# First layer of a two-layer backbone: ten more first-product blocks made in the gate stage (80 spilled in place of 70), the loop projects that many fewer

## The chip, the cores and the metric

The kernel runs on one core of one Trainium2 chip. Its time is the device time of one execution in microseconds (us), given as the median of several runs. Engines are named as the profile names them: PE is TensorE, DVE is VectorE, ACT is ScalarE, POOL is GpSimd and SP is SyncE, which here only issues transfers.

## The reference, cut to what matters

Two layers act on 512 latent tokens and 256 context tokens of width 1024. Each layer has a token mixer (convolution, gating and attention heads, one output projection) and then a channel mixer that looks up experts; the change lies in the channel mixer of the first layer. There every token picks 16 of 16,384 experts for each of 8 heads, and

```
a   = gelu(einsum('tkd,td->tk', u_tab[ec], xc))    # first product: picked rows of u times the token
out = einsum('tk,tkd->td', a * gc, v_tab[ec])      # second product: gated sum of the picked rows of v
```

where `ec` holds the 128 picked experts of a token and `gc` their softmax gates.

## The kernel before, in words

For the 512 latent tokens of the first layer the kernel computes both products for all experts and not for the picked ones: the 16,384 experts are 128 blocks of 128, and a dense matrix of gates, zero where an expert was not picked, takes the place of the lookup. The 256 context tokens are done by lookup. For each of 512 jobs one indirect transfer on POOL (line 842) gathers 128 rows of 4 KB, and DVE multiplies or accumulates them (lines 847 and 858).

A **first product** (`u_phase`, line 828) is one block of 128 experts times all 512 tokens. SP loads 512 KB of `u`, ACT splits off the high part (line 163, tile `whi`), DVE makes the low part (line 164, `wlo`), PE runs 24 matmuls (lines 315 to 317), and ACT applies the gelu (line 831, tile `a`). For a block that is to be spilled ACT's queue then sends `a`, 256 KB, to the DRAM tensor `ad`.

The channel mixer of the layer has three stretches. In the **lead-in** the tail of the expert choice (many small DVE instructions) runs beside first products. In the **gate stage** 32 steps build the dense gates: in each, DVE makes two one-hot tiles (lines 989 and 990, `oj` and `oi`) and two weighted ones (line 994, `wo`), PE runs 32 short matmuls (line 1002), ACT evicts them twice (line 1004), and 1 MB goes to the DRAM tensor `gd`. First products run between the steps. In the **loop**, 16 groups of 8 expert blocks pass. For each block `prep` (line 1042) needs `a`: a spilled one is read back from `ad`, one of the three carried ones (`CARRY`) is still on the chip, any other is a first product made now. DVE multiplies it with the gates (line 1056), ACT and DVE split it (lines 1061 and 1062), and PE runs 8 second products of 24 matmuls for the group (lines 1098 to 1100), after each of which DVE adds into the stream (line 1101, `x_l`). The gates of the next group, 2 MB, are read from `gd` once in a group.

Which blocks are spilled is worked out from `AHEAD`: as many of the 128 as it says, evenly spread. Spilled and carried blocks are made in this order by `upto` (line 898), which is called in the expert choice (20 blocks, `AHP`) and after every gate step, up to `AHP` and then a share of `AHT` that grows with the step to the power 1.3 (line 1010). The same call hands out the gather jobs, 112 before the loop. The 400 that are left are handed out in the loop by `pace` (line 1030) in proportion to steps, of which a second product counts one and a first product two (`PWU`).

Loads of `u` and `v` and the gathers take their buffers in turn from one ring of raw tiles, 6 in lead-in and gate stage and 9 in the loop; `whi` and `wlo` have three buffers each. A scheduler then puts the instructions of each engine in an order of its own, by a simulated timeline; it is this order that runs, and it is not the order of the program text.

Of the kernel before, what the change touches and what calls it, by code (L numbers as in the profile page):

```python
# [49 lines left out]
NGATH = [2, 1]  # L50
GT = 16
TI = 2
AHEAD = [70, 62]
AHP = [20, 24]
AHT = [53, 41]
TKP = [16, 0]
TKT = [96, 0]
TKE = [0, 0]
# [19 lines left out]
def kernel(ctx: ExitStack, tc: tile.TileContext, a):  # L78
# [728 lines left out]
    gv = gd[:, :L * NKEYS].rearrange("p (b i t) -> p b i t", i=NKEYS, t=GT)  # L807
    ad = dram.tile([max(AHEAD), P, L], F32, name="ad")

    def peer(l, last, G, h_):  # L810
        e0 = l * NKEYS * NKEYS
        with ExitStack() as es:
# [7 lines left out]
            for i in range(NKEYS):  # L820
                if (i + 1) * AHEAD[l] // NKEYS > i * AHEAD[l] // NKEYS:
                    order[i] = len(order)
# [75 lines left out]
            def upto(nu, nt):  # L898
                while nxt[0] < min(nu, len(early)):
                    kept[early[nxt[0]]] = u_phase(early[nxt[0]])  # L900
                    nxt[0] += 1
                tick(nt - done[0])
# [43 lines left out]
            with ExitStack() as es1:  # L946
# [16 lines left out]
                with ExitStack() as es2:  # L963
# [10 lines left out]
                    for it in range(td):  # L974
# [10 lines left out]
                        for tb in range(P // GT):  # L985
# [23 lines left out]
                            j = it * (P // GT) + tb + 1  # L1009
                            upto(AHP[l] + int(AHT[l] * (j / ntb) ** QU[l]), TKP[l] + int(TKT[l] * (j / ntb) ** QT[l]))  # L1010
                    upto(NKEYS, 0)

            with ExitStack() as es2:
# [11 lines left out]
                ng = NKEYS // GS  # L1025
                nstep = (NKEYS - AHEAD[l] - CARRY) * PWU[l] + NKEYS - PEND[l]
                rest = len(jobs) - done[0]
# [187 lines left out]
```

## Time and profile before

| | us |
|---|---|
| median of 3 runs | 3820.23 |
| lowest and highest of them | 3800.05, 3831.27 |
| the profiled execution's own time | 3811.28 |
| its span, first to last instruction | 3809.5 |

The profile is of one execution. A busy share is the part of a stretch in which an engine executed something; matmuls overlap, so PE's work is better counted from the number of matmuls and the distance between two starts. "PEclk" is the granted clock of TensorE as a share of full speed. In a row of the chain, the timeline or the groups, the part behind "<-" in brackets names what ended an engine's idle time.

### The profile page before, as it was taken

To read this page: it belongs to the slowest core of one execution; us is meant where nothing else is said; L and a number is where in the kernel's file an instruction comes from. 1 tells how busy PE (TensorE), PEld (TensorE's weight loads), DVE (VectorE), ACT (ScalarE), POOL (GpSimd) and SP (SyncE) were. 2 spreads that over 40 slices of the span, in tenths; PEclk is the share of its full clock that TensorE was granted. 3 is DMA by queue.
4 is the path that set the end of the run, shared out by engine and by line. 5 is a ranking of instruction groups with operands and counts; after the bars stand their busy time and mean duration, and the time that the engine had idled before them with its cause. 6 is when DMAs were issued, how large, how long until landed. Compare 5 with 4: busy or idle time off the path is not lost.

```text
span 3809.5 us, 52565 instructions
## 1 busy us (share of the span) xinstructions
PE 3557.1 (93%) x18725; PEld 2986.6 (78%) x18725; DVE 3204.5 (84%) x6734; ACT 1488.4 (39%) x2115; POOL 1070.9 (28%) x806
## 2 busy tenths in 40 slices
PE   8989889999997999999999989889999899999998
PEld 4767768877775877778787777669999788888887
DVE  7966899988897888989999878649999588888887
ACT  4255432223664222323222233633368333333333
POOL 0000000143333545555455500000000244444441
PEclk8989889999998999999999999889999999999999
DMA  7711235588987999999999937014467899999995
GB/s 246 229 59 52 62 117 165 175 297 282 333 316 274 345 344 332 346 339 362 340 329 339 329 134 270 10 62 132 132 224 280 286 345 340 347 347 347 341 351 193
DMA packets 377663, 967.04 MB, mean 254 GB/s; under 512 B 30632, under 2 KB 160472, under 8 KB 369848
## 3 DMA queue, kind: packets, MB, share of 16 engines
q1 hardware_dynamic: 239048, 468.13, 36.0%
q0 software_dynamic: 111280, 406.28, 29.9%
q10 hardware_dynamic: 27072, 89.27, 5.9%
q8 instruction: 147, 2.41, 0.2%
q14 instruction: 116, 0.95, 0.1%
HBM read 872.20 MB, written 91.36 MB: 253 GB/s over the span
## 4 chain that ended last, share of the span: by engine, by line
PE 58%; issue 14%; DVE 9%; DMA 8%; POOL 7%; ACT 3%; POOLq 0%; SPq 0%; ACTq 0%; DVEq 0%
PE mm L315 10%; PE mm L317 10%; PE mm L316 10%; PE sc L1082 9%; POOL raw L842 7%; PE tp L1082 4%; DMA raw<-in_u_n_dram,E 3%; PE sc L1098 2%; PE sc L1099 2%; PE sc L1100 2%; DMA raw<-in_v_n_dram,E 2%; DVE wlo L164 2%; PE sc L1002 1%; PE mm L596 1%; PE tp L591 1%
## 5 line engine op out<-in xcount | busy, mean ns | idle before, releaser
L163 ACT ACTIVATE whi<-raw 128x1024 fp32r<-128x1024 f32 x640 | 676.1, 1059 | 1530.6 <-PE mm L316 629.7
L842 POOL DMA_INDIRECT raw<-in_u_n_dram,E x384 | 523.5, 1363 | 1753.0 <-DVE wlo L164 841.2
L317 PE MATMUL mm<-hi_l,wlo 128*128 128x512 f32 (+1 forms) x2656 | 989.1, 372 | 11.9 <-DVE wlo L164 11.9
L315 PE MATMUL mm<-hi_l,whi 128*128 128x512 f32 (+1 forms) x2656 | 995.3, 375 | 5.1 <-ACT hi_l L294 2.5
L316 PE MATMUL mm<-lo_l,whi 128*128 128x512 f32 (+1 forms) x2656 | 989.3, 373 | 3.3 <-DVE lo_l L295 3.2
L164 DVE TENSOR_TENSOR wlo<-raw,whi 128x1024 fp32r<-128x1024 f32 x640 | 779.8, 1220 | 168.0 <-ACT whi L163 162.8
L842 POOL DMA_INDIRECT raw<-in_v_n_dram,E x384 | 530.8, 1382 | 518.6 <-DVE ht L858 275.2
L317 PEld LDWEIGHTS mm<-hi_l,wlo 128*128 128x128 f32 x2656 | 502.5, 189 | 80.9 <-DVE wlo L164 15.4
L315 PEld LDWEIGHTS mm<-hi_l,whi 128*128 128x128 f32 x2656 | 502.4, 189 | 76.0 <-ACT hi_l L294 4.8
L316 PEld LDWEIGHTS mm<-lo_l,whi 128*128 128x128 f32 x2656 | 502.8, 189 | 74.8 <-DVE lo_l L295 7.0
L847 DVE SCALAR_TENSOR_TENSOR raw<-raw,ht 128x1024 f32<-128x1024 f32 x384 | 465.2, 1220 | 111.2 <-DMA raw<-in_u_n_dram,E 110.5
L858 DVE SCALAR_TENSOR_TENSOR ht<-raw,wg,ht 128x1024 f32<-128x1024 f32 x381 | 488.1, 1281 | 25.2 <-DMA raw<-in_v_n_dram,E 22.4
L1098 PE MATMUL sc<-ahi,whi 128*128 128x512 f32 x1024 | 400.3, 398 | 30.1 <-DVE x_l L1101 15.8
L1099 PE MATMUL sc<-alo,whi 128*128 128x512 f32 x1024 | 406.5, 398 | 17.4 <-DVE alo L1062 16.8
L1100 PE MATMUL sc<-ahi,wlo 128*128 128x512 f32 x1024 | 404.0, 395 | 0.5 <-DVE wlo L164 0.5
L1061 ACT ACTIVATE ahi<-a 128x512 fp32r<-128x512 f32 (+1 forms) x256 | 144.7, 576 | 348.9 <-DVE a L1056 348.7
L1098 PEld LDWEIGHTS sc<-ahi,whi 128*128 128x128 f32 x1024 | 194.5, 191 | 82.8 <-DVE x_l L1101 22.2
L1099 PEld LDWEIGHTS sc<-alo,whi 128*128 128x128 f32 x1024 | 195.2, 191 | 69.4 <-DVE alo L1062 30.1
L1004 ACT ACTIVATE gs<-sc 128x1024 f32<-128x1024 f32 x112 | 213.9, 2018 | 66.2 <-PE sc L1002 62.9
L1100 PEld LDWEIGHTS sc<-ahi,wlo 128*128 128x128 f32 x1024 | 195.2, 191 | 41.6 <-DVE wlo L164 1.4
L1056 DVE TENSOR_TENSOR a<-a,gt 128x512 f32<-128x512 f32 (+1 forms) x256 | 156.7, 619 | 47.1 <-DMA gt<-gd 26.5
L1062 DVE TENSOR_TENSOR alo<-a,ahi 128x512 fp32r<-128x512 f32 (+1 forms) x256 | 155.8, 619 | 15.2 <-ACT ahi L1061 15.0
(313 smaller groups left out, 4804.8 us busy)
## 6 DMA issues: line engine op xcount, KB each, us to landing
raw<-in_u_t_dram SPq DMA_DIRECT2D x256, 512.0 KB, 5.6
raw<-in_v_b_dram SPq DMA_DIRECT2D x128, 512.0 KB, 6.8
raw<-in_v_n_dram SPq DMA_DIRECT2D x128, 512.0 KB, 6.1
gd<-gs ACTq DMA_DIRECT2D x56, 1024.0 KB, 4.9
raw<-in_w_adt_dram SPq DMA_DIRECT2D x64, 512.0 KB, 4.3
gt<-gd SPq DMA_DIRECT2D x15, 2048.0 KB, 13.9
raw<-in_wq_dram SPq DMA_DIRECT2D x48, 512.0 KB, 3.6
gt<-gd SPq DMA_DIRECT2D x15, 1536.0 KB, 14.1
```

The source lines that it names most:

```text
L163: nc.scalar.activation(hi, raw, AF.Copy)
L164: nc.vector.tensor_tensor(lo, raw, hi.bitcast(F32), op=ALU.subtract)
L315: nc.tensor.matmul(ps, whi[:, k], hhi[:, k], start=(k == 0), stop=False)
L316: nc.tensor.matmul(ps, whi[:, k], hlo[:, k], start=False, stop=False)
L317: nc.tensor.matmul(ps, wlo[:, k], hhi[:, k], start=False, stop=(k == K - 1))
L842: nc.gpsimd.indirect_dma_start(out=g, out_offset=None, in_=tab, in_offset=bass.IndirectOffsetOnAxis(ap=G["E"][:, it, k:k + 1], axis=0), el ...
L847: nc.vector.scalar_tensor_tensor(g, g, 1.0, G["ht", it], op0=ALU.mult, op1=ALU.mult, accum_out=G["dots", it][:, k:k + 1])
L858: nc.vector.scalar_tensor_tensor(G["acc", it], g, G["wg", it][:, k:k + 1], G["acc", it], op0=ALU.mult, op1=ALU.add)
L1082: nc.tensor.matmul(accs[t][h], w[:, sl], v[:, halves[h]], start=(i == 0 and j == 0), stop=(i == NKEYS - 1 and j == 2))
L1098: nc.tensor.matmul(ps, vh[:, c], wh, start=(c == 0), stop=False)
L1099: nc.tensor.matmul(ps, vh[:, c], wl, start=False, stop=False)
L1100: nc.tensor.matmul(ps, vl[:, c], wh, start=False, stop=(c == GS - 1))
```

## The change

Two numbers of the first layer change, both from the same table. The layer spills 80 blocks in place of 70, and the gate stage is to hand out 63 first products in place of 53; the second entry of each table belongs to the second layer and stays.

```
-AHEAD = [70, 62]
+AHEAD = [80, 62]
 AHP = [20, 24]
-AHT = [53, 41]
+AHT = [63, 41]
```

`nstep`, by which the loop hands out the gather jobs, falls from 232 to 212, since it is worked out from `AHEAD` (line 1026). `ad` grows from 70 to 80 blocks.

The scheduler moves more than the table says. These are the rows of PE where the gate stage meets the loop, before (`oj` and `wo` are the gate step's tiles, `sc` is the PSUM tile, `ahi` and `alo` a split first product, `whi` and `wlo` a split block of `v`):

```order
L1002 LDWEIGHTS oj_11584
L1002 MATMUL sc_11611<-wo_2349_11590,oj_11584 128x128
L1098 MATMUL sc_11847<-ahi_11752,whi_11843 128x512
L1099 MATMUL sc_11847<-alo_11753,whi_11843 128x512
L1100 MATMUL sc_11847<-ahi_11752,wlo_11844 128x512
```

Ahead of these stand 6 whole gate steps with no other matmul between them, and the last first product lies before those. The same place in the change:

```order
L315 MATMUL mm_12043<-hi_l_5686,whi_12039 128x512
L316 MATMUL mm_12043<-lo_l_5687,whi_12039 128x512
L317 MATMUL mm_12043<-hi_l_5686,wlo_12040 128x512
L1098 MATMUL sc_12147<-ahi_12092,whi_12143 128x512
L1099 MATMUL sc_12147<-alo_12093,whi_12143 128x512
L1100 MATMUL sc_12147<-ahi_12092,wlo_12144 128x512
L1098 MATMUL sc_12182<-ahi_12092,whi_12178 128x512
```

Three whole first products now stand between the last gate matmul and the first second product, and matmuls of first products stand between all of the 32 gate steps. Counted over the whole order, 83 first products stand ahead of the first second product (74 before), and in the loop each of the first 15 groups has three and the last none, 45 in all (54 before, of them one to five in a group).

These are the rows of DVE at the same place, before:

```order
L994 TENSOR_TENSOR wo_2328_11464<-oi_11461,wh_10713 128x2048
L994 TENSOR_TENSOR wo_2329_11466<-oi_11461,wh_10713 128x2048
L989 TENSOR_TENSOR oj_11584<-iota_1769_8102,ij_10709 128x2048
L990 TENSOR_TENSOR oi_11585<-iota_1769_8102,ij_10709 128x2048
L994 TENSOR_TENSOR wo_2348_11588<-oi_11585,wh_10713 128x2048
L994 TENSOR_TENSOR wo_2349_11590<-oi_11585,wh_10713 128x2048
L1056 TENSOR_TENSOR a_11662<-a_11662,gt_5797 128x512
L1056 TENSOR_TENSOR a_11756<-a_11756,gt_5797 128x512
```

And with the change (`raw`, `dots` and `ht` are those of a gather job):

```order
L994 TENSOR_TENSOR wo_2399_11930<-oi_11925,wh_10951 128x2048
L847 SCALAR_TENSOR_TENSOR raw_12070,dots_120<-raw_12070,ht_4_119 128x1024
L164 TENSOR_TENSOR wlo_11850<-raw_11847,whi_11849 128x1024
L847 SCALAR_TENSOR_TENSOR raw_12073,dots_120<-raw_12073,ht_4_119 128x1024
L847 SCALAR_TENSOR_TENSOR raw_12076,dots_120<-raw_12076,ht_4_119 128x1024
L164 TENSOR_TENSOR wlo_11884<-raw_11881,whi_11883 128x1024
L847 SCALAR_TENSOR_TENSOR raw_12173,dots_120<-raw_12173,ht_4_119 128x1024
L164 TENSOR_TENSOR wlo_11974<-raw_11971,whi_11973 128x1024
```

Behind the last gate instruction stand 9 gather jobs and 6 low parts before the first multiplication with gates, where before none stood. Ahead of the first gate instruction there are 10 gather jobs and 3 low parts fewer. In the last stretch the order repeats a low part and two gather jobs.

## Rows read from the trace of the kernel before

**Rows 1.** The head of the page.

```profile
span 3809.5 us, 52565 instructions
PE 3557.1 (93%) x18725; PEld 2986.6 (78%) x18725; DVE 3204.5 (84%) x6734; ACT 1488.4 (39%) x2115; POOL 1070.9 (28%) x806
```

**Rows 2.** Sums by stretch: its length, then each engine's busy us and instructions.

```profile
core 0: us, PE busy (x) PEld busy (x) DVE busy (x) ACT busy (x) POOL busy (x), PEclk, DMA share, GB/s
747.00:922.90 175.90, 159.94 (x669) 128.20 (x667) 153.91 (x408) 47.00 (x65) 72.35 (x55) 0.95 0.87 289
922.90:1160.00 237.10, 221.42 (x1582) 180.50 (x1581) 208.83 (x230) 153.02 (x145) 78.11 (x47) 0.99 0.90 318
1160.00:1191.70 31.70, 15.81 (x161) 14.16 (x161) 23.79 (x25) 20.68 (x17) 0.00 (x0) 0.72 0.55 221
747.00:1160.00 413.00, 381.35 (x2249) 308.70 (x2247) 362.74 (x637) 200.02 (x209) 150.46 (x102) 0.98 0.89 306
1191.70:2258.40 1066.70, 1022.98 (x4389) 826.14 (x4390) 931.58 (x1146) 300.51 (x388) 543.81 (x389) 0.98 0.90 325
```

**Rows 3.** Timeline of PE: start, length, instruction; the second matmul is the 19th after the first.

```profile
699.77 0.39 PE L316 MATMUL mm<-lo_l,whi 128*128 128x512 f32 x1
...
704.08 0.39 PE L317 MATMUL mm<-hi_l,wlo 128*128 128x512 f32 x1
...
1056.88 1.96 PE L1002 MATMUL sc<-wo,oj 128*128 128x128 f16 x31
1058.65 0.48 PE L316 MATMUL mm<-lo_l,whi 128*128 128x512 f32 x1
```

**Rows 4.** The same sums by group of the loop (9 of 16 groups, then 14 together).

```profile
1191.70:1263.90 72.20, 65.83 (x264) 52.49 (x265) 61.23 (x93) 20.72 (x27) 39.40 (x28) 0.91 0.91 328
1263.90:1325.60 61.70, 60.66 (x265) 49.32 (x264) 51.07 (x78) 16.58 (x21) 30.29 (x23) 1.00 0.90 317
...
1465.80:1529.20 63.40, 61.31 (x266) 49.20 (x265) 53.55 (x80) 16.90 (x21) 31.04 (x24) 1.00 0.91 333
...
1600.00:1660.70 60.70, 60.18 (x266) 49.52 (x265) 57.24 (x60) 17.24 (x22) 38.76 (x25) 1.00 0.98 360
...
1732.00:1804.20 72.20, 71.01 (x313) 58.46 (x312) 71.14 (x74) 21.58 (x28) 44.53 (x32) 1.00 0.99 372
...
2004.40:2068.30 63.90, 61.03 (x266) 49.22 (x265) 58.25 (x60) 16.65 (x21) 37.05 (x26) 1.00 0.95 343
...
2140.50:2206.50 66.00, 62.02 (x265) 50.45 (x264) 57.10 (x60) 17.25 (x21) 34.62 (x22) 0.97 0.91 330
2206.50:2258.40 51.90, 50.82 (x228) 41.49 (x228) 31.74 (x61) 17.98 (x30) 0.00 (x0) 1.00 0.12 44
1263.90:2206.50 942.60, 906.33 (x3899) 732.16 (x3898) 838.61 (x996) 261.81 (x331) 504.41 (x361) 0.99 0.94 340
```

**Rows 5.** Waits in those 14 groups: us in total, times, longest.

```profile
ACT whi L163 <- PE sc L1099: 353.8, 89, 8.1
```

**Rows 6.** Timeline of DVE: gate step, low part, gather job, then the loop's start.

```profile
1090.74 1.22 DVE L989 TENSOR_TENSOR oj<-iota,ij 128x2048 f16<-128x2048 f16 x1
1091.87 1.22 DVE L164 TENSOR_TENSOR wlo<-raw,whi 128x1024 fp32r<-128x1024 f32 x1
1093.01 1.22 DVE L847 SCALAR_TENSOR_TENSOR raw<-raw,ht 128x1024 f32<-128x1024 f32 x1
...
1190.27 3.10 DVE L1056 TENSOR_TENSOR a<-a,gt 128x512 f32<-128x512 f32 x5 [7.74 <-ACT gt L1007]
...
1211.34 1.41 DVE L1101 SCALAR_TENSOR_TENSOR x_l<-sc,mods,x_l 128x512 f32<-128x512 f32 x2
```

**Rows 7.** Timeline of PE where the gate stage ends.

```profile
1191.67 0.79 PE L1098 MATMUL sc<-ahi,whi 128*128 128x512 f32 x1 [4.28 <-ACT ahi L1061]
```

**Rows 8.** Transfers issued between 747 and 2258.4: times, KB each, us to landing.

```profile
raw<-in_u_t_dram SPq DMA_DIRECT2D x107, 512.0 KB, 6.4
...
ad<-a ACTq DMA_DIRECT2D x53, 256.0 KB, 5.9
```

## The prediction

> **What bounds the kernel now.** Read the head of the page first: PE is busy for 93% of the span and DVE for 84% [rows 1]. A mean over the program decides nothing here, so the second thing to read is the sums by stretch. From 747 to 2258 us PE, DVE and the transfer engines are all near full, and none of them alone sets the pace: in the loop the shares are 96%, 87% and 90% [rows 2]. The pace of PE comes from the timeline: nineteen matmuls of a first product start 4.31 us apart in all, 0.227 us each, so a first product of 24 is 5.44 us of PE; 31 gate matmuls take 1.77 us to the next start, 0.057 us each [rows 3]. By these the loop's 4389 matmuls are 995 us of work in 1066.7 us, a rate of 93%. From 747 to 1160 there are 2249 matmuls, 864 of them of the gate (27 of the 32 steps): 1385 x 0.227 + 864 x 0.057 = 363 us of work in 413 us, 88%. From 1160 to 1191.7 PE does only the last 160 gate matmuls, at a granted clock of 0.72 of full, so between its two levels of 1.2 and 2.4 GHz [rows 2]. In the loop ACT's longest wait is for PE to give back a buffer of split weights, 353.8 us [rows 5]: weights lie ready, and PE mostly leads.
>
> The third view is the same sum by group. A group is 192 matmuls of second products and 24 for each first product in it. The five groups with three (265 matmuls) take 61.7, 63.4, 60.7, 63.9 and 66.0 us, 63.1 in the mean; the 14 groups after the first take 942.6 us, 67.3 each, with some 50 first products in them, (3899 - 14 x 192) / 24 = 50.5 by the row, which holds a few other matmuls [rows 4].
>
> **The change part by part.** The table says ten first products more ahead of the loop; the order says nine, since one of the loop's stood ahead already. Of those nine, eight leave the 14 groups (50 to 42) and one the last group; group 0 keeps three.
>
> *Lead-in and gate stage, until the first second product.* Added on PE: 9 x 5.44 = 49 us. On DVE 9 low parts of 1.14 us, 10 us [rows 6]. On ACT nine splits and gelus, beside a busy time of 153 us in 237 [rows 2]: hidden. Transfers: nine loads of 512 KB and ten or so spills of 256 KB [rows 8], about 7.2 MB, which at the stretch's 318 GB/s [rows 2] is 23 us. Nothing of the 49 us can be less than nothing, because the work stays on the same engine; all of it could be hidden, since from 747 to 1191.7 PE has 73 us without work (444.7 less 363 less 9 for the last 160 gate matmuls). So the ends are 0 and +49. The work ahead of the loop becomes 363 + 9 + 49 = 421 us. At today's 88% that is 478 us, which ends 34 us later than 1191.7; at the loop's 93% it is 453 us, 8 us later. What speaks for the better rate: the bare stretch of 31.7 us is filled, the low clock with it, and DVE, which has 128 gate instructions and some 50 gather jobs there [rows 6], gets little more. What speaks for the worse: loads and gathers share six raw buffers in this stretch against nine in the loop, and near its end the order runs one low part and two gather jobs in turn. I take **+27 us**, nearer the upper end.
>
> *The hand-over.* Before, PE waits 4.28 us for the first second product [rows 7], and the two blocks that are made first end at 1211.34 [rows 6], 19.7 us after it, where their 48 matmuls are 10.9 us of work. With the change three first products cover the wait, but the low part of the third block of `v` needs a buffer that the last first product frees, and behind it DVE has 13 short instructions of 0.60 us, which is what five take in 3.01 us, and 7 gather jobs of 1.22 us [rows 6]. With the low part that is 17.5 us, and the high part ahead of it on ACT adds about as much as a low part: 19 us. One delay takes the place of the other: **0**; if the cover is gone, +4 us.
>
> *The 14 groups.* Removed: eight first products. PE alone: 8 x 5.44 = 44 us, or 64.2 us a group. But the gather jobs stay, and are handed out in fewer steps. The five groups with three first products issued 24.0 of them on POOL, the mean of the 14 is 25.8 [rows 4]; 1.8 more at 1.22 us of DVE make 63.1 + 2.2 = 65.3 us. Transfers: 942.6 us at 340 GB/s are 320 MB; eight loads fewer and eight read-backs more leave 318. At 360 GB/s, the best of the five, this is 63.1 us a group; at the present 340 it is 66.9. The ends are therefore 14 x 63.1 = 883 (-59) and 14 x 66.9 = 937 (-6). I take 65.2 us, where the sums by DVE and by transfers meet (349 GB/s): 913, **-30 us**.
>
> *The last group.* One first product fewer, no gather job left in it (POOL 0) [rows 4]: **-5 us**. The second layer's order is that of before, 0.
>
> A rule to weigh: the rows show the transfer engines at 0.94 over the 14 groups, and at 0.99 in the one with five first products, which moved 372 GB/s [rows 4]. So traffic has some room, but not much. The Trainium skill, "DMA: Bandwidth & Descriptors", section "Issuing engines are not separate DMA queues", says that transfers started by SP, ACT and POOL all run on the same 16 engines and interleave. By it a spill on ACT's queue is not free beside the gathers, and where the transfers set the pace of both stretches the sum would be that of the second rival. The trace's rows can't tell yet, as all three engines are near full.
>
> Sum: 27 + 0 - 30 - 5 = -8 us. The profiled execution took 3811.28 us, its span 3809.5 [rows 1]; it lies 9 us below the median of the three runs, 3820.23. Against its own time the sum gives 3803; for the median I forecast **3812 us**, no change that can be told. Its own range is 3790 to 3838.
>
> **The rivals.** *PE alone is the bound* (13%). Then the filled stage runs at 93% (+8), and the groups lose PE's 44 us, the last one 5: -41, 3779. For it: the waits for buffers that PE holds [rows 5], and groups with three first products at 60.7 and 61.7 us. Against: those had fewer gather jobs, 24.0 for 25.8 [rows 4], and DVE and the transfers have no room to follow.
>
> *The transfers set both stretches* (15%). The stage grows by the 23 us of its 7.2 MB, the groups keep 340 GB/s (-6), the last group gives 5: +12, 3832. For it: shares of 0.90 and 0.94. Against: 360 and 372 GB/s in single groups.
>
> *Slower: six raw buffers in the gate stage* (12%). In the lead-in 55 gathers and some 28 loads (669 matmuls by 24) went through six buffers in 175.9 us [rows 2], 12.7 us for a buffer's turn. Near the end of the stage the change has three transfers for each first product of 5.44 us, which six buffers can serve if a turn is below 10.9 us. From there on the buffers decide: at 12.7 a first product takes 6.4 us, and eight of them cost 7 us more. Nothing of the 49 us is hidden then. With the loop at 340 GB/s: 49 + 7 - 6 - 5 = +45, 3865. Against: the first products of the lead-in ran at about that pace beside the expert choice, which is over by then.
>
> *The change does not move what it says*: the order shows nine moved, so it has no chance of its own.
>
> **How the numbers follow.** About 1% of the time, 38 us, is what a measurement can tell from no change; below 3782 is faster and above 3858 slower. The forecast has 60%, nearly all of it within. Of the first rival most is faster, and a little of the forecast: 15%. Of the third rival some two thirds are slower, and a little of the others: 10%. The rest, 75%, is the same. The range, 3772 to 3850, takes in the first rival and the second, and leaves out the far ends and most of the third.
>
> **What the next profile would show.** The first second product comes at 1200 to 1226 us, not at 1191.7, about 1219; the last gate steps run with the clock at full, without the 0.72. The 14 groups take about 65.2 us each and differ less than 61 to 78, at about 349 GB/s; the last group takes 47 us. The forecast is wrong if the groups come at 63 us or less, then PE alone was the bound, or if they stay at 67 and the first second product comes after 1235, then buffers and transfers were. It is also wrong if the second layer's stretches change by more than a few us.

## The result: 0.75% slower, inside the range but not as forecast

The change takes **3847.5 us** in the median of 6 runs (3835.4 to 3855.3), the kernel before 3814.0 in 6 runs beside it; the ratio is **1.0075, 95% interval 1.0057 to 1.0094**. Forecast were 3812 us and a gain of 8; it became a loss, inside the wide range (3772 to 3850) that was to take in the rivals too, and outside the forecast's own (3790 to 3838). The profiled execution took 3835.4 us, its span is 3833.6, which is 24.1 more than that of before; the sums below are made against these two spans. It was the fastest of the six, so some 9 us of the loss in the medians stand in no row below, and a difference of a few us in one row is not clear of the 20 us by which the six differ.

The head of the page, against [rows 1], shows nothing of it: the shares are the same to 1%.

```profile
span 3833.6 us, 52638 instructions
PE 3559.0 (93%) x18725; PEld 2980.1 (78%) x18725; DVE 3203.4 (84%) x6734; ACT 1487.3 (39%) x2115; POOL 1050.3 (27%) x806
```

The sums by stretch and by group of the changed kernel do, which answer to [rows 2] and [rows 4]. The columns are those of [rows 2]; the first row ends with the first gate matmul, the fifth is group 0, the sixth the 14 groups, the last the last group.

```profile
747.00:898.70 151.70, 141.28 (x603) 113.58 (x602) 135.96 (x374) 42.15 (x58) 52.12 (x44) 0.97 0.84 280
898.70:1160.00 261.30, 248.26 (x1758) 203.44 (x1758) 227.85 (x243) 170.19 (x162) 73.56 (x44) 0.98 0.88 305
1160.00:1196.60 36.60, 33.07 (x188) 26.89 (x186) 15.36 (x19) 15.53 (x17) 7.65 (x5) 0.95 0.69 237
1196.60:1221.40 24.80, 18.35 (x77) 14.44 (x74) 10.12 (x15) 5.91 (x7) 9.10 (x8) 0.93 0.77 255
1221.40:1300.20 78.80, 65.56 (x265) 51.57 (x266) 64.14 (x98) 19.73 (x26) 33.31 (x28) 0.87 0.92 321
1300.20:2235.90 935.70, 870.21 (x3707) 695.94 (x3706) 833.37 (x995) 251.99 (x318) 494.13 (x363) 0.99 0.95 343
2235.90:2283.00 47.10, 45.28 (x204) 36.95 (x203) 28.82 (x57) 15.87 (x27) 0.00 (x0) 1.00 0.07 25
```

| part | before | change | difference | forecast |
|---|---|---|---|---|
| to the first second product | 1191.7 | 1221.4 | **+29.7** | +27 |
| group 0 | 72.2 | 78.8 | **+6.6** | 0 |
| the 14 groups | 942.6 | 935.7 | **-6.9** | -30 |
| last group | 51.9 | 47.1 | **-4.8** | -5 |
| from there to the end | 1551.1 | 1550.6 | -0.5 | 0 |

Two of the terms came as forecast, and the second layer did not move. Of the time to the first second product, the lead-in became 24 us shorter (first gate matmul at 898.7, before at 922.9) and the stage behind it 54 us longer. Group 0 and above all the 14 groups did not come as forecast. In those 14 groups PE was busy 870.2 us in place of 906.3, so 36 us of its work are gone, and the groups are 6.9 us shorter. DVE's 833.4 us are nearly the 838.6 of before, and the granted clock is 0.99 in both. ACT's longest wait there, for buffers that PE holds, is still long against [rows 5]:

```profile
ACT whi L163 <- PE sc L1099: 331.6, 81, 6.1
```

So weights still lie ready for PE, and yet it stands still for 65 of the 935.7 us.

### The profile page after: what moved, and what is told of

The parts are those of the page before. It is cut to its first block, busy times and chain, and to the rows that moved or that the text cites. A ratio compares the mean times of both kernels' runs of the same rounds, so it can differ in the third digit from the quotient of the medians.

```text
span 3833.6 us, 52638 instructions
## 1 busy us (share of the span) xinstructions
PE 3559.0 (93%) x18725; PEld 2980.1 (78%) x18725; DVE 3203.4 (84%) x6734; ACT 1487.3 (39%) x2115; POOL 1050.3 (27%) x806
## 3 DMA queue, kind: packets, MB, share of 16 engines
q1 hardware_dynamic: 240488, 470.75, 36.3%
## 4 chain that ended last, share of the span: by engine, by line
PE 59%; issue 13%; DVE 11%; DMA 8%; POOL 5%; ACT 3%; SPq 0%; ACTq 0%; POOLq 0%; DVEq 0%
PE mm L315 10%; PE mm L316 10%; PE mm L317 10%; PE sc L1082 9%; POOL raw L842 5%; PE tp L1082 4%; PE sc L1098 3%; PE sc L1099 3%; PE sc L1100 3%; DMA raw<-in_u_n_dram,E 2%; DVE wlo L164 2%; DVE ht L858 2%; DVE xr L220 1%; PE mm L596 1%; PE tp L591 1%
## 5 line engine op out<-in xcount | busy, mean ns | idle before, releaser
L317 PE MATMUL mm<-hi_l,wlo 128*128 128x512 f32 (+1 forms) x2656 | 989.3, 373 | 14.0 <-DVE wlo L164 13.9
L842 POOL DMA_INDIRECT raw<-in_u_n_dram,E x384 | 505.5, 1317 | 1810.7 <-DVE wlo L164 862.6
L858 DVE SCALAR_TENSOR_TENSOR ht<-raw,wg,ht 128x1024 f32<-128x1024 f32 x381 | 487.3, 1279 | 26.5 <-DMA raw<-in_v_n_dram,E 24.1
L1098 PEld LDWEIGHTS sc<-ahi,whi 128*128 128x128 f32 x1024 | 194.0, 191 | 96.9 <-ACT ahi L1061 36.3
```

Source lines behind the costliest of these rows:

```text
L317: nc.tensor.matmul(ps, wlo[:, k], hhi[:, k], start=False, stop=(k == K - 1))
L842: nc.gpsimd.indirect_dma_start(out=g, out_offset=None, in_=tab, in_offset=bass.IndirectOffsetOnAxis(ap=G["E"][:, it, k:k + 1], axis=0), el ...
L858: nc.vector.scalar_tensor_tensor(G["acc", it], g, G["wg", it][:, k:k + 1], G["acc", it], op0=ALU.mult, op1=ALU.add)
L1098: nc.tensor.matmul(ps, vh[:, c], wh, start=(c == 0), stop=False)
```

## Where the gain of the 14 groups went

A group has two parts with different limits. The **hand-over** runs from the last second product of the group before to the last split of this one (`alo`, line 1062): PE makes first products there and begins the first of the second products, each of which needs all eight splits. The **rest** is the other second products. These are the sums over the 14 hand-overs, and then over the 14 rests, of the kernel before: the length, then busy time of each engine, in us, and means.

```profile
sum 404.80, PE 384.31 PEld 306.99 DVE 382.10 ACT 143.20 POOL 212.34; mean PE 27.45 PEld 21.93 DVE 27.29 ACT 10.23 POOL 15.17
...
sum 538.30, PE 522.52 PEld 425.56 DVE 457.73 ACT 119.66 POOL 294.64; mean PE 37.32 PEld 30.40 DVE 32.70 ACT 8.55 POOL 21.05
```

And of the change:

```profile
sum 357.70, PE 306.02 PEld 233.78 DVE 343.89 ACT 121.99 POOL 179.21; mean PE 21.86 PEld 16.70 DVE 24.56 ACT 8.71 POOL 12.80
...
sum 578.00, PE 564.18 PEld 462.15 DVE 487.19 ACT 129.77 POOL 319.28; mean PE 40.30 PEld 33.01 DVE 34.80 ACT 9.27 POOL 22.81
```

Before, both engines were full in the hand-overs: PE for 95% and DVE for 94% of 404.8 us. The change takes 78 us of PE's busy time out of the hand-overs, but only 38 of DVE's. They shorten by 47, and now DVE is full (96%) while PE is busy for 86%. In the rests PE is the full one in both kernels (97% and 98%), and 42 us of its work came to lie there: the new order puts one of a group's three first products into the rest. The rests grow by 40. In all PE's busy time falls by 36.6 us, and its time without work grows by 29.2 (404.8 + 538.3 - 906.8 = 36.3 before, 357.7 + 578.0 - 870.2 = 65.5 now), and all of that in the hand-overs (20.5 before, 51.7 now).

One hand-over in the timeline of DVE shows how full it is: start, length, instruction. A row without brackets began without a wait.

```profile
1775.53 1.29 DVE L1056 TENSOR_TENSOR a<-a,gt 128x512 f32<-128x512 f32 x2
1776.73 1.28 DVE L858 SCALAR_TENSOR_TENSOR ht<-raw,wg,ht 128x1024 f32<-128x1024 f32 x1
1777.93 0.68 DVE L1056 TENSOR_TENSOR a<-a,gt 128x512 f32<-128x512 f32 x1
1778.53 0.68 DVE L1062 TENSOR_TENSOR alo<-a,ahi 128x512 fp32r<-128x512 f32 x1
1779.13 1.28 DVE L858 SCALAR_TENSOR_TENSOR ht<-raw,wg,ht 128x1024 f32<-128x1024 f32 x1
1780.33 1.28 DVE L1062 TENSOR_TENSOR alo<-a,ahi 128x512 fp32r<-128x512 f32 x2
```

PE meanwhile waits for splits, one after another:

```profile
1777.53 0.73 PE L1098 MATMUL sc<-ahi,whi 128*128 128x512 f32 x2 [0.87 <-ACT ahi L1061]
1779.27 0.50 PE L1099 MATMUL sc<-alo,whi 128*128 128x512 f32 x1 [1.00 <-DVE alo L1062]
```

DVE goes from one instruction to the next, gather jobs of 1.2 us between multiplications and splits of 0.6, and PE takes each split as it comes. Counted over the 14 groups, a hand-over of the change has 9.1 whole gather jobs, 3.1 low parts and most of the eight multiplications and splits on DVE, and DVE waits for 1.0 us of its 25.6.

## The experiments

Times are medians, ratios are to the kernel before on the same chip, with the 95% interval. "V0" is the start of the first second product; "groups" the 14 groups together; they, the waits and the busy times come from one profiled execution each. Unless said otherwise an experiment is the change with one edit. The scheduler makes a new order for every edit, so the order of DVE and PE in the loop differs in places between any two of these kernels, and not only in the line that is shown.

### Is it the bytes?

**e1**, half of each gathered row (the other half's products are replaced by a repeat, so the picked experts' sums are not the reference's), and **e3**, the same edit in the kernel before.

```
-nc.gpsimd.indirect_dma_start(out=g, ..., in_=tab, ...
+nc.gpsimd.indirect_dma_start(out=g[:, :D // 2], ..., in_=tab.rearrange("n (a d) -> (n a) d", a=2), ...
```

> The change, with each of the first layer's 512 gathers moving half a row (256 KB in place of 512 KB) while DVE works on as many elements as before (the half is read twice, so the result is another one). In the change 14 groups of the loop take 66.8 us each, of which 59.8 us are PE's work, and the first second product starts at 1221.4 us. If the transfers' rate sets the groups (theory 1), they fall to 61 to 63 us, since 26 gathers move 6.8 MB less of 22.8 MB a group. If DVE's queue at the start of a group sets them (theory 2), they stay at 65 to 67 us. If in the gate stage the turn of the six raw buffers is what counts, a shorter transfer brings the first second product to about 1200 to 1210 us.

> The kernel before, with half the bytes of a gather as in the run beside it. Its 14 groups take 67.3 us with 63.2 us of PE work in the mean. Theory 1: about 64 us, and the change (run beside it) is then 2 to 3 us a group faster than this. Theory 2: 66.5 to 67.5 us.

e1: 3798.7 us, 0.9961 (0.9945 to 0.9977); V0 at 1213.0, groups 921.2. Traffic in the 14 groups fell from 343 to 246 GB/s, and the groups by 14.5 us, to 65.8 each where theory 1 asked for 61 to 63. e3: 3795.2 us, 0.9958 (0.9937 to 0.9979); V0 at 1154.5, groups 968.4, which is longer than with whole rows and which neither theory has. The rate of the transfers does not set the groups: the rival "transfers set both stretches" gave nearly the number that came (-6) for a cause that is not there.

### Is it DVE's work?

**e2**, DVE's arithmetic on a gathered row cut to 128 of 1024 columns (the rest of the sums is left out), **e4** the same in the kernel before, and **e13** with 896 columns.

```
-nc.vector.scalar_tensor_tensor(g, g, 1.0, G["ht", it], ...
+nc.vector.scalar_tensor_tensor(g[:, :w], g[:, :w], 1.0, G["ht", it][:, :w], ...     # w = 128, or 896; line 858 alike
```

> The change, with the gathers whole but DVE's arithmetic on them cut to 128 of 1024 columns in the first layer (the rest of the lookup is left out). Theory 1 (transfers): groups stay at 65 to 67 us, because bytes are the same. Theory 2 (DVE's queue): 26 jobs a group lose about 1.0 us each, the wait for split first products at the start of a group goes, and groups fall to 60.5 to 62.5 us. Gate stage: DVE is not its limit by either, the first second product stays within 8 us of 1221; only if DVE is the limit it comes 20 us or more earlier.

> The kernel before, with DVE's arithmetic on the gathers cut to 128 columns. Theory 1: 66.5 to 67.5 us a group. Theory 2: 63.5 to 65 us, near PE's work of 63.2, and the change under the same cut 3 us a group faster, as eight first products of 5.44 us over 14 groups.

> The change, but DVE's work on a gathered row takes 896 of 1024 columns (1/8 of the picked experts' sums for the context tokens is left out, so that part of the output is not the reference's); transfers and the number of instructions stay. 363 jobs in the 14 groups become shorter by 0.13 us: 48 us less DVE work, 833 to some 785. Theory 'queue' (DVE's instructions and waits one behind another set the 14 groups): the groups come 40 to 50 us down, one for one, 886 to 896, while PE's own 59.8 us a group (837) leaves that room. Rival 'order of PE and DVE together' (each waits for the other at fixed places): less than half of it, 912 to 935.

e2: 3775.3 us, 0.9899 (0.9816 to 0.9981); V0 1213.5, groups 877.4. e4: 3727.6 us, 0.9773 (0.9700 to 0.9847); V0 1137.2, groups 910.6. Hand-overs and rests of e2:

```profile
sum 312.00, PE 299.18 PEld 233.47 DVE 219.43 ACT 119.22 POOL 127.31; mean PE 21.37 PEld 16.68 DVE 15.67 ACT 8.52 POOL 9.09
...
sum 565.30, PE 560.53 PEld 458.64 DVE 296.67 ACT 133.72 POOL 262.07; mean PE 40.04 PEld 32.76 DVE 21.19 ACT 9.55 POOL 18.72
```

And of e4:

```profile
sum 366.20, PE 360.72 PEld 296.27 DVE 245.25 ACT 143.21 POOL 151.44; mean PE 25.77 PEld 21.16 DVE 17.52 ACT 10.23 POOL 10.82
...
sum 544.40, PE 533.19 PEld 435.87 DVE 276.02 ACT 119.63 POOL 241.22; mean PE 38.09 PEld 31.13 DVE 19.72 ACT 8.55 POOL 17.23
```

With DVE relieved, PE is busy for 96% of the hand-overs of the change and 99% of those of before, and **the change's groups are 33 us shorter than those of before (877.4 against 910.6)**, where they were 6.9 shorter with DVE's whole work. In a group that is 62.7 against 65.0 us, 2.4 apart where the expectation had 3. The saved work of PE is real; with DVE's whole work it is lost again. That is the result of this study that stands firmest, though the two orders differ in more than the eight first products. As a whole the change loses even so: 3775.3 against 3727.6 us, since its first second product comes 76 us later than that of before (1213.5 against 1137.2) once DVE is relieved.

e13: 3811.6 us, 0.9998 (0.9980 to 1.0016); DVE's work falls by 41.5 us (833.4 to 791.9), the groups by 20.4 (to 915.3). That is just under half, and inside the 912 to 935 of the rival, in which PE and DVE wait for each other at fixed places; one for one does not hold in this direction. DVE's waits for PE in the groups grew, from 37 to 86 us, which fits a hand-over that became shorter ahead of a rest that PE sets.

The dose in the other direction is the next one.

### Is the first hand-over the gather jobs that stand in it?

**e8**, the pace of the gather jobs begins 20 steps later.

```
-int(rest * step[0] / nstep)
+int(rest * (step[0] - 20 * (l == 0)) / (nstep - 20 * (l == 0)))
```

> The change, with no gather job handed out in the first 20 steps of the loop (the 400 are spread over the rest), so that fewer stand ahead of the first multiplications with gates. If gather jobs that wait for their transfers on DVE make the hand-over slow, the matmul loss at the start of group 0 falls from 18.9 us to 11 or less and the two first second products take under 21 us (29 in the change, 19.7 before). Theory 2 for the rest: the 27 jobs put off cost the later groups 1.22 us of DVE each, so the groups rise by about 2 us and the whole is no faster than the change; if DVE does not set them, the whole is 8 us faster.

3861.8 us, 1.0134 (1.0092 to 1.0175). Group 0 falls from 78.8 to 63.7 us, so the gather jobs in it set its length. The edit takes away 27 of its 30, where before has 25, so what the 6.6 us themselves are is read from the timelines. In the change PE stood still from 1225.2 to 1236.9. Timeline of PE of the change:

```profile
1221.39 0.50 PE L1098 MATMUL sc<-ahi,whi 128*128 128x512 f32 x1 [3.45 <-ACT ahi L1061]
...
1224.39 0.80 PE L1100 MATMUL sc<-ahi,wlo 128*128 128x512 f32 x1 [0.56 <-DVE wlo L164]
1236.95 1.22 PE L1098 MATMUL sc<-ahi,whi 128*128 128x512 f32 x2 [11.76 <-ACT ahi L1061]
```

and DVE, which had to multiply the next block before ACT could split it, was at its gather jobs (the last row is its first two adds into the stream):

```profile
1228.30 1.22 DVE L164 TENSOR_TENSOR wlo<-raw,whi 128x1024 fp32r<-128x1024 f32 x1
1229.43 0.68 DVE L1056 TENSOR_TENSOR a<-a,gt 128x512 f32<-128x512 f32 x1
1231.64 1.23 DVE L847 SCALAR_TENSOR_TENSOR raw<-raw,ht 128x1024 f32<-128x1024 f32 x1 [1.53 <-DMA raw<-in_u_n_dram,E]
...
1234.40 1.23 DVE L847 SCALAR_TENSOR_TENSOR raw<-raw,ht 128x1024 f32<-128x1024 f32 x1 [1.52 <-DMA raw<-in_u_n_dram,E]
...
1250.27 1.41 DVE L1101 SCALAR_TENSOR_TENSOR x_l<-sc,mods,x_l 128x512 f32<-128x512 f32 x2
```

The first add starts 28.9 us after the first second product, before 19.7 us after it ([rows 6] and [rows 7]), and in e8 some 14. The granted clock takes part in that: it stands at half, 1.2 GHz, from 1222.5 to 1243.0, after a stretch of 24.8 us in which PE was busy for 18.4, and behind the long wait matmuls start 0.43 us apart and not 0.227. Over group 0 it is 0.87 in the change, 0.91 before and 1.00 in e8.

But the jobs come later: some 28 more in the 14 groups, DVE's work there +33.7 us, the groups +35.4 (971.1). Here DVE's work counts one for one.

### Do fewer gather jobs in the loop give the gain back?

**e5**, 128 as the gate stage's share of gather jobs in place of 96, **e6** the same in the kernel before, **e7** the table's step in the other direction.

```
-TKT = [96, 0]                       -AHEAD = [80, 62]   -AHT = [63, 41]
+TKT = [128, 0]     (e5, e6)         +AHEAD = [60, 62]   +AHT = [43, 41]     (e7)
```

> The change, with 32 gather jobs more handed out in the gate stage (144 before the loop in place of 112) and so 368 in place of 400 in the loop; nothing else. If DVE's queue sets the groups (theory 2): 32 x 1.22 = 39 us of DVE leave the loop, its 14 groups fall from 66.8 to 64 to 65 us (-25 to -39 us), while in the gate stage DVE stood idle 68 us for gathers and PE sets the end, so the first second product moves by +15 us at most: the whole comes out 10 to 35 us faster than the change (3847), near 3815 to 3835. If the six raw buffers set the gate stage, 32 more transfers at 12.7 / 6 = 2.1 us each make it up to 67 us longer, and the whole is slower than the change.

> The kernel before with the same 32 jobs moved. There the gate stage was the shorter by 54 us when DVE's arithmetic was cut, so DVE set its end: theory 2 expects the first second product 25 to 40 us later and the groups 25 to 39 us shorter in all, the whole within 15 us of before (3812).

> The step of the change taken the other way from before: 60 spilled and 43 first products handed out in the gate stage. Theory 2 (DVE sets gate stage and loop in the kernel before, first products cost it 1.14 us each): first second product 10 to 20 us earlier than 1191.7, groups at 67.5 to 69.5 us since PE's work rises to about 65.5 of them, last group +10: whole 0 to +30 us against before. If PE alone set the loop, the groups would rise by 2.5 x 1 us in PE work and keep the loss of 4.4: 70 us, and the whole +35 or more.

e5: 3853.3 us, 1.0102 (1.0071 to 1.0134); V0 1203.0, but groups 981.4. e6: 3921.4 us, 1.0275 (1.0235 to 1.0315); V0 1207.0, groups 1053.9. e7: 3902.7 us, 1.0229 (1.0187 to 1.0271); V0 1173.8, groups 1056.9. In all three the groups came out 70 us or more longer than any expectation had them. That DVE's work alone decides falls by e5: it is 35 us less there (798.5) and the groups are 46 longer. DVE waits. Its waits in the 14 groups of the change, in us in total, times, longest:

```profile
DVE x_l L1101 <- PE sc L1100: 37.3, 30, 3.4
DVE raw L847 <- DMA raw<-in_u_n_dram,E: 27.8, 21, 3.5
DVE ht L858 <- DMA raw<-in_v_n_dram,E: 19.7, 11, 4.4
```

and of e5:

```profile
DVE ht L858 <- DMA raw<-in_v_n_dram,E: 97.9, 41, 5.9
DVE x_l L1101 <- PE sc L1100: 54.6, 33, 4.2
DVE raw L847 <- DMA raw<-in_u_n_dram,E: 13.7, 9, 2.1
```

### Is it the number of raw buffers?

**e9**, 8 buffers in the loop's ring; **e11**, 10, at the cost of one stash tile; **e10**, five in the gate stage with nine left in the loop.

```
-RXB = 3     -bufs=RXB  bufs=STB                     -RAWB = 6  RXB = 3
+RXB = 2     +bufs=RXB + 1  bufs=STB - 1 (layer 1)   +RAWB = 5  RXB = 4
   (e9)          (e11)                                  (e10)
```

> The change, but the raw buffers that the loop adds to the six are two in place of three: loads and gathers take turns in a ring of 8 in the loop. The gate stage is untouched. In the change the 14 groups take 935.7 us, in which 112 loads of v, 42 of u and 363 gathers, 517 transfers, go through 9 buffers: a buffer's turn is 16.3 us. Theory 'ring' (what DVE waits for when it waits for gathered rows is the turn of the ring): if a turn stays 16.3 us, the groups come to 1053 us (+117); at the least DVE's waits for gathers (47.5 us in the change) double, groups +40 or more. Theory 'queue' (DVE's own instructions set the groups, the waits are only a matter of order): work stays at about 833 us, groups within 10 us of 935.7.

> The change with a loop ring of 10 raw buffers in place of 9 in the first layer; the room comes from the stash of first products, 4 tiles in place of 5 there. Theory 'ring': DVE waits less for gathered rows (47.5 us in the 14 groups of the change, down to some 20), groups 905 to 915, time 20 to 30 us less. Theory 'queue': work 833 us and order decide, groups within 10 us of 935.7. If the smaller stash is a limit of its own the groups are longer by both.

> The change with five raw buffers in lead-in and gate stage in place of six, and four added in the loop in place of three, so that the loop's ring has 9 as before. It asks what sets the gate stage of the change, where shorter gather work on DVE won only 8 us (the first second product at 1213.5 for 1221.4). Theory 'ring': the stage from the first gate matmul (898.7) to the first second product (1221.4) is set by the turn of its buffers, in part or wholly: wholly would be 322.7 x 6 / 5 = 387, the first second product 65 us later; in part 20 to 40. Rival 'PE and the gate steps' (a first product and a gate step follow each other in PE's order and their waits are short): later by less than 10. The 14 groups stay within 10 us of 935.7 by both.

The constants of e9 and e10 are those of both layers, so their second layer changed too: from the last group on, e9 is 8.8 us longer than the change and e10 11.7 shorter. e9: 3849.2 us, 1.0097 (1.0076 to 1.0117), groups 938.9; e11: 3905.1 us, 1.0245 (1.0222 to 1.0267), groups 989.3, DVE's waits for gathered rows 106 us; e10: 3827.9 us, 1.0050 (1.0025 to 1.0074), V0 1234.3, groups 926.4. A buffer fewer does nothing to the groups, so it is not the count: the theory falls. e11 can't speak for the count: it has a stash tile less as well, and longer groups were expected by both theories if that tile counts. In the gate stage one fewer costs 13 us, between the two expectations, and clear of the 2 us by which e8 and e9, whose stage is that of the change, differ from it; whether buffers set that stage stays open.

### What makes DVE wait for gathered rows?

The orders of these kernels differ in many places, and one difference can be counted. A gather can be issued only when DVE has passed the instruction that frees its buffer, and its rows land some 7 us after the issue (7.5 and 6.6 us in the median in the change, for rows of `v` and of `u`). For each gather of the 14 groups I summed, in the order, DVE's work between that point and the gather's own job, with POOL's issues taken as 1.4 us apart (they take 1383 ns in the mean for rows of `v`). What that work has over 7 us is the **lead**; where it has less, DVE must wait for the difference, the shortfall. The work itself is 8 to 11 us in the mean. The mean lead, the sum of the shortfalls, and the waits measured in gather jobs, each over the 14 groups:

| | lead, us | shortfalls, us | waits, us |
|---|---|---|---|
| e6, e7, e5, e11 | 1.0, 1.5, 1.9, 2.9 | 293, 208, 153, 141 | 181, 152, 116, 106 |
| e8, change, e10 | 3.9, 3.5, 3.3 | 74, 49, 45 | 36, 49, 41 |
| e13, before, e12, e9 | 2.8, 3.1, 2.9, 2.7 | 30, 27, 27, 26 | 10, 35, 30, 31 |

The mean alone does not sort them, as e11 and e12 show. The shortfalls sort the three rows, though not the kernels within a row, and they come out too large where the waits are long. The expectations name a mean lead by another count, whose steps are not on record: 4.8 us in the change, 2.5 in e14, -1.0 in e5, 7.4 in e15 and 9.5 in e16, where the count above has 3.5, 2.5, 1.9, 4.3 and 4.9.

From the lead **e14** (112 in the table of e5), **e15** (the same with a longer free end) and **e16** (84 spilled) were forecast.

```
-TKT = [96, 0]     -PEND = [6, 4]                  -AHEAD = [80, 62]   -AHT = [63, 41]
+TKT = [112, 0]    +PEND = [20, 4]  (e15, e16)     +AHEAD = [84, 62]   +AHT = [67, 41]   (e16)
```

> The change with 128 gather jobs handed out before the loop in place of 112; 350 in place of 362 in the 14 groups. Theory 'lead': a gather can be issued only when DVE has passed the instruction that frees its buffer, nine turns of the ring before, and its rows land some 7 us later; in this order DVE has 2.5 us of work in the mean between that point and the job (4.8 in the change, -1.0 where 32 jobs were moved early). So DVE's waits for gathered rows come out between those two: 47.5 us in the change, 119 with 32 early, here 70 to 110, and the groups at 935 to 965 though DVE's work falls by 14. Theory 'queue without lead': groups 915 to 925, waits some 47.

> As the one before (128 gather jobs ahead of the loop, 350 in the 14 groups), but the pace of the others counts 20 steps at the end as free and not 6, so they are handed out a little sooner all along and the order leaves DVE 7.4 us of work in the mean between the point where a gather's buffer comes free and its job, in place of 2.5. The same number of jobs, the same buffers and transfers. Theory 'lead': waits for gathered rows 15 to 40 us, groups 900 to 922. Without it: as the one before, within 10 us.

> 84 blocks spilled and 67 first products in the gate stage, 128 gather jobs ahead of the loop, 20 free steps: four first products fewer in the loop than in the change, 351 gather jobs in the 14 groups, and a lead of 9.5 us in the mean. Theory 'lead and queue': waits for gathered rows below 25 us, DVE's work 818, groups 885 to 910; the first second product 10 to 25 us later than 1221.4 for four more first products. Time 3800 to 3835. If the waits stay at 47 us or above the theory of the lead is wrong.

e14: 3854.3 us, 1.0109 (1.0072 to 1.0145), groups 956.0. Its waits:

```profile
DVE ht L858 <- DMA raw<-in_v_n_dram,E: 76.3, 35, 7.1
DVE x_l L1101 <- PE sc L1100: 24.5, 22, 3.2
DVE raw L847 <- DMA raw<-in_u_n_dram,E: 19.0, 21, 2.2
```

e15: 3843.4 us, 1.0078 (1.0039 to 1.0116), groups 935.3:

```profile
DVE x_l L1101 <- PE sc L1100: 53.8, 37, 3.4
DVE wlo L164 <- ACT whi L163: 27.8, 12, 6.5
DVE raw L847 <- DMA raw<-in_u_n_dram,E: 10.7, 10, 3.2
...
DVE ht L858 <- DMA raw<-in_v_n_dram,E: 2.8, 5, 0.9
```

The waits for rows came near what was expected, 96 us and then 13.5, with nearly the same jobs (350 and 347) and the same buffers; in e16 they are 9 us. The shortfalls are 98, 9 and 1 us. With e17 and e18 below, where the ring has 7, they are 25 and 101 us and the waits 42 and 69. So the order, by how far it puts a job behind the point that frees its buffer, accounts for most of these waits. The times that I had derived from it did not come: the groups of e15 are 21 us shorter than those of e14 and not 40, those of e16 (3856.1 us, 1.0126, 1.0086 to 1.0166, V0 1245.5) are 936.1 in place of 885 to 910, with four first products fewer. DVE then waits for PE (54 and 56 us) and, in e16, 35 us for the next gates. The waits for rows are a cost where the work ahead of a job is short; they are not what holds the change's groups at 66.8 us.

### Can the hand-over itself be shortened?

**e12**, the splits' low part on POOL. **e17**, four blocks of the next group split before the group's end in place of two, with 12 pairs of split tiles and a ring of 7, and **e18**, the same in the kernel before.

```
-nc.vector.tensor_tensor(lo, A, hi.bitcast(F32), op=ALU.subtract)
+nc.gpsimd.tensor_tensor(lo, A, hi.bitcast(F32), op=ALU.subtract)      (e12, first layer)

-EXC = [{6: (0,), 7: (1,)}, ...     vps: bufs=4, 6     RXB 3
+EXC = [{4: (0,), 5: (1,), 6: (2,), 7: (3,)}, ...     vps: bufs=6, 6     RXB 1      (e17, e18, first layer)
```

> The change, but the low part of every split first product of the first layer (alo, 128 a layer, 112 of them in the 14 groups, 0.6 us each on DVE) is made on POOL. Theory 'queue' (DVE's instructions one behind another set the groups): DVE's work falls by 67 us from 833 to some 766, the groups come down towards PE's 837 plus a start loss, as with the short gather work (877): 875 to 900, -35 to -60, and the time falls by about as much. Rival (POOL is late instead): a low part stands in POOL's queue between gathers, they are issued later, DVE's waits for gathered rows grow by what its work fell: groups within 15 us of 935.7 or longer.

> The change, but four blocks of the next group (not two) are multiplied and split before the group's last second product: 12 pairs of split first products in place of 10, paid for with two raw buffers (a ring of 7 in the loop), and the order's preparing of blocks 0 to 3 after the products 4 to 7. Theory 'hand-over of the groups': in the change the last of a group's 8 splits stands 21 us of DVE work behind the last add of the group before, and PE waits 6.9 us a group for it; here it stands 15 us behind. The wait falls to 1 to 3 us, the 14 groups from 935.7 to 865 to 900 us, the time by 30 to 65. Theory 'queue' (DVE's work and waits for rows set the groups whatever is split first): the groups stay within 15 us of 935.7. The smaller ring may lengthen DVE's waits for gathered rows (47.5 us in the change); by the lead in the order (7.4 us against 4.8) they should not grow.

> The kernel before with the same: 12 pairs, four blocks ahead, a ring of 7 in the loop. The last split stands 19 us of DVE work behind the last add of the group before (24 in the kernel before). Theory 'hand-over of the groups': PE's wait falls from 3.7 us a group to 1 or 2, the 14 groups from 942.6 to 905 to 925; with the hand-over relieved in both, the change's eight first products fewer show: its groups are 25 to 45 us shorter than these. Theory 'queue': the two differ by 5 to 10 us, as the change and the kernel before do.

e12: 3915.6 us, 1.0276 (1.0253 to 1.0298), groups 997.7, and DVE's work rose to 863.5 us although 112 instructions had left it (the last section tells why). The rival's late rows are not it: the waits for rows fell to 30 us, and those for PE grew to 97. e17: 3904.5 us, 1.0243 (1.0220 to 1.0266), groups 981.1. Its hand-overs and rests:

```profile
sum 275.70, PE 229.22 PEld 172.62 DVE 263.36 ACT 89.01 POOL 155.98; mean PE 16.37 PEld 12.33 DVE 18.81 ACT 6.36 POOL 11.14
...
sum 705.20, PE 664.91 PEld 535.67 DVE 564.75 ACT 161.34 POOL 375.67; mean PE 47.49 PEld 38.26 DVE 40.34 ACT 11.52 POOL 26.83
```

The hand-overs shortened as the order said, from 25.6 to 19.7 us each, and DVE is full in them again (96%). The first products moved into the rests, and there weights came late, as these two waits of ACT for loads show (1.4 and 23.4 us in the change):

```profile
ACT whi L163 <- DMA raw<-in_u_t_dram: 126.7, 16, 19.4
ACT whi L163 <- DMA raw<-in_v_b_dram: 104.1, 38, 15.3
```

I read this as the price of a ring of 7, but it was not tried with the old ring. e18: 3878.8 us, 1.0174 (1.0143 to 1.0204), groups 1009.6, with the same late weights and 52 us of waits for gates. The two could not tell what they were made for. None of the 13 kernels that do the whole computation is faster than the kernel before.

## Why the prediction was wrong, point by point

- **Gate stage, +27: right** (+29.7). I took the stage near its old rate of 88%; the work of 421 us took 474 (1221.4 - 747), 89%. The bare 31.7 us with a clock of 0.72 are gone, the clock stands at 0.95 and 0.93 there. Why the rate stays is only half known: DVE's gather work set the stage of before (e4: 54 us earlier without most of it) and no longer sets that of the change (e2: 8 us earlier). So the number is in part luck: no reason that I gave is shown to be the one.
- **The hand-over to the loop, 0: wrong** (+6.6 in group 0). The three first products did not cover the first wait: PE still stood still for 3.45 us ahead of the first second product (4.28 before [rows 7]), which the first part of the table holds. Behind it I counted 7 gather jobs and 13 short instructions once, ahead of the third block; the order goes on with gather jobs between the next splits too, and two of them waited 1.5 us each for their rows. The first add came 28.9 us after the first second product in place of 19.7. e8 shows that the gather jobs set this group; which part of the 6.6 us is theirs and which the clock's (0.87 for 0.91) is not shown.
- **The 14 groups, -30: wrong** (-6.9), and this is the step that failed. It put "63.1 + 2.2 = 65.3 us" on a group, from five groups with three first products and 1.8 gather jobs more. The rows at hand said otherwise: DVE was busy 51.1, 53.6, 57.2, 58.3 and 57.1 us in those five, 55.4 in the mean, and 838.6 / 14 = 59.9 in all [rows 4]. So DVE had 4.5 us less to do in them than in the mean, not 2.2. Less the eight low parts that go, 0.7 us a group, that makes 63.1 + 3.8 = 66.9 us, and 66.8 came. That sum takes DVE's work one for one, which e8 bears out and e13 does not, so that it comes so near is in part luck. The deeper fault is the mean over a group: in it PE (96%) looks like the bound [rows 4], and ACT's waits for PE [rows 5] are the rests', where that is so. In the hand-overs, from which the removed matmuls came, DVE was as full as PE (382 and 384 of 404.8 us), and of the 44 us of PE's work that were removed the groups gave 6.9; with DVE relieved in both kernels they give 33 (e2, e4).
- **The last group, -5, and the second layer, 0: right.** No gather job stands in that group, so PE's saving comes out nearly whole, 4.8 of 5.44 us.
- **Transfers.** The rule I weighed, from the Trainium skill, "DMA: Bandwidth & Descriptors", section "Issuing engines are not separate DMA queues", says that all issuing engines share the 16 engines. No run here speaks against it, but e1 shows that the share of 0.95 was not the bound.
- **The rivals.** "PE alone" would have needed groups of 64.2 us; only with DVE relieved they come to 62.7. "Six raw buffers" priced V0 at some 1248 and it came at 1221.4. Of the second sign of being wrong only half came: the groups stayed near 67 us, but V0 did not come after 1235, and so the sign does not name the cause.

**What stays open:** what sets the pace of the changed gate stage; why 41 us less of DVE's work gives only 20 (e13) where 34 more cost 35 (e8); how much of the 6.9 us is the spread of single executions; and whether a shorter hand-over pays when the weights' ring keeps its size.

## What to carry to other kernels

When two engines are both near full, cut the period at the points where one hands results to the other and read who is full in each piece: work that is taken from an engine in a piece that the other one sets is given back as idle time. When comparing groups of unequal content, set every engine's busy time beside the length, not only that of the engine you change. And with an order written ahead of time, count how much work the consuming engine has between the instruction that frees a buffer and the one that needs its refill: where it is less than the transfer takes, the engine waits, in e6 at 289 GB/s for 181 us where the change waits 49 at 343.

## What the runs showed of the hardware that was not expected

In e12 the subtraction on POOL took 1677 ns where DVE takes 684, and DVE's own instructions slowed meanwhile. DVE of the change from 1312 to 2240 us (count, busy us, mean ns, idle before):

```profile
L858 DVE SCALAR_TENSOR_TENSOR ht<-raw,wg,ht 128x1024 f32<-128x1024 f32 x254 | 324.9, 1280 | 21.4 <-DMA raw<-in_v_n_dram,E 19.7
...
L1101 DVE SCALAR_TENSOR_TENSOR x_l<-sc,mods,x_l 128x512 f32<-128x512 f32 x112 | 82.5, 746 | 37.3 <-PE sc L1100 37.3
L1056 DVE TENSOR_TENSOR a<-a,gt 128x512 f32<-128x512 f32 x112 | 75.0, 685 | 4.1 <-DMA a<-ad 4.1
```

DVE and POOL in e12, from 1312 to 2240 us too:

```profile
L858 DVE SCALAR_TENSOR_TENSOR ht<-raw,wg,ht 128x1024 f32<-128x1024 f32 x227 | 322.0, 1419 | 3.0 <-DMA raw<-in_v_n_dram,E 0.3
...
L1056 DVE TENSOR_TENSOR a<-a,gt 128x512 f32<-128x512 f32 x105 | 97.3, 944 | 1.7 <-DMA a<-ad 1.7
L1101 DVE SCALAR_TENSOR_TENSOR x_l<-sc,mods,x_l 128x512 f32<-128x512 f32 x104 | 77.0, 748 | 87.0 <-PE sc L1100 86.9
```

```profile
L1062 POOL TENSOR_TENSOR alo<-a,ahi 128x512 fp32r<-128x512 f32 x105 | 174.9, 1677 | 8.6 <-ACT ahi L1061 6.3 <-issue 1.2
```

A multiplication with the gates went from 685 to 944 ns in the mean, a gather job on rows of `v` from 1280 to 1419. The slow ones are those that ran beside a subtraction on POOL: 47 multiplications that overlap one by more than 0.2 us took 1263 ns in the mean, 30 that overlap none 687; 73 gather jobs took 1710 ns, 146 took 1281. POOL's gather issues do not do this: 127 of those 146 ran beside one. The Trainium skill, "GPSIMD Engine Reference", section "Key points", says that POOL shares its SBUF interfaces with DVE and that DVE instructions with two SBUF inputs contend. The rows agree: both of these read two tiles from SBUF, and the add into the stream, which reads one of its two from PSUM, stayed at 748 ns (746 in the change), also the 8 times that it ran beside a subtraction.
